# A quarter-row first load ahead of a streamed row sum

## Chip, cores and metric

One core of a Trainium2 chip. The metric is the device time of one execution in microseconds, the median of several runs of each kernel. The "span" of a profile (from the first to the last instruction of the program) is shorter than the time by about 1.4 us.

## The reference

```python
def reference(x):                       # x: 32 x 512 x 1024, float32
    relu_x = np.maximum(x, 0)
    return np.sum(relu_x, axis=-1)      # 32 x 512
```

64 MiB (67.11 MB) come in, 64 KB go out. There are 16,384 rows of 4 KB, 128 for each of the 128 SBUF partitions.

## The kernel before

Each partition owns 112 consecutive rows of a first region (pitch from partition to partition: 448 KB) and 16 rows of a second. The 112 rows arrive in seven chunks of 16 rows, 64 KB per partition, in three rotating buffers. All loads go through one queue, that of SyncE (SP). The first chunk is split into a one-row load and a fifteen-row load, and both are issued ahead of the barrier with which the program starts.

```python
CHUNKS = [[(0, 0, 1), (0, 1, 15)]] + [[(0, 16 * c, 16)] for c in range(1, 7)]
...
for c in range(NBIG + 1):
    if c >= NB:
        sp.wait_ge(s_dve, done[c - NB])       # buffer free again
    if c < NBIG:
        i = 0
        for g, j, n in CHUNKS[c]:
            sp.dma_start(
                out=buf[:, c % NB, i : i + n, :], in_=xv[g][:, j : j + n, :]
            ).then_inc(s_in[c], 16)
            i += n
            if c == 0:                        # moved ahead of the start barrier
                code.insert(arrival, code.pop())
                arrival += 1
... # tail loads of 8, 4, 2 rows and four pieces of the last two rows, then the first store
for c in range(NTWO):
    act.wait_ge(s_in[c], 16 * len(CHUNKS[c])) # for chunk 0: both loads
    ... # ScalarE applies ReLU in place, VectorE reduces along the row
```

## Time and profile before

| | before |
|---|---|
| median time, 6 runs | 161.05 us (160.93 to 161.22) |
| span of the profiled run | 159.5 us |
| load queue's share of 16 engines' span | 98.1% |
| VectorE / ScalarE busy | 76% / 64% |
| second load: landing after its issue | 21.3 us |

Two lines of the list of issues in the profile of the kernel before matter (columns: how many, KB, us from issue to landing):

```profile
buf<-in_x_dram SPq DMA_DIRECT2D x1, 7680.0 KB, 21.3
...
buf<-in_x_dram SPq DMA_DIRECT2D x1, 512.0 KB, 3.6
```

The first load is 128 packets of 4 KB, one per partition, eight for each of the 16 engines. The second is 128 packets of 60 KB, again eight per engine. These two lines are what the change resizes. The page, the chain and the windows follow in the prediction.

### The profile page before, as it was taken

To read this page: it belongs to the slowest core of one execution; us is meant where nothing else is said; L and a number is where in the kernel's file an instruction comes from. 1 tells how busy PE (TensorE), PEld (TensorE's weight loads), DVE (VectorE), ACT (ScalarE), POOL (GpSimd) and SP (SyncE) were. 2 spreads that over 40 slices of the span, in tenths; PEclk is the share of its full clock that TensorE was granted. 3 is DMA by queue.
4 is the path that set the end of the run, shared out by engine and by line. 5 is a ranking of instruction groups with operands and counts; after the bars stand their busy time and mean duration, and the time that the engine had idled before them with its cause. 6 is when DMAs were issued, how large, how long until landed. Compare 5 with 4: busy or idle time off the path is not lost.

```text
span 159.5 us, 149 instructions
## 1 busy us (share of the span) xinstructions
DVE 120.5 (76%) x59; ACT 101.5 (64%) x54; POOL 0.2 (0%) x4
## 2 busy tenths in 40 slices
DVE  0000000009999999999999999999999999898985
ACT  3000059990699808996099951999329980496975
POOL 0000000000000000000000000000000000000000
DMA  9969996996997998979969969969969979798994
GB/s 378 493 293 447 493 526 263 526 526 263 526 477 312 526 427 362 526 312 477 526 296 493 526 263 526 526 263 526 526 263 526 460 329 526 320 468 374 415 403 142
DMA packets 2449, 67.18 MB, mean 421 GB/s; under 512 B 528, under 2 KB 784, under 8 KB 1168
## 3 DMA queue, kind: packets, MB, share of 16 engines
q1 hardware_dynamic: 2448, 67.18, 98.1%
q14 instruction: 1, 0.01, 0.0%
HBM read 67.11 MB, written 0.07 MB: 421 GB/s over the span
## 4 chain that ended last, share of the span: by engine, by line
DVE 55%; DMA 34%; ACT 9%; SPq 2%; issue 0%
DVE res L156 54%; DMA buf<-in_x_dram 34%; ACT buf L141 9%; SPq L101 1%; SPq L112 1%; DVE buf L126 0%; DVE seam L126 0%; SPq L91 0%
## 5 line engine op out<-in xcount | busy, mean ns | idle before, releaser
L156 DVE TENSOR_REDUCE res<-buf 128x4 f32<-128x4096 f32 (+3 forms) x19 | 99.5, 5308 | 35.6 <-ACT buf L141 35.6
L141 ACT ACTIVATE buf<-buf 128x7168 f32<-128x7168 f32 (+5 forms) x13 | 80.4, 6233 | 46.2 <-DMA buf<-in_x_dram 46.2
L123 ACT ACTIVATE buf<-buf 128x1024 f32<-128x1024 f32 (+2 forms) x19 | 18.9, 998 | 8.9 <-DMA buf<-in_x_dram 8.9
L126 DVE TENSOR_SCALAR_CACHE_REDUCE buf<-buf 128x1024 f32<-128x1024 f32 (+2 forms) x19 | 20.7, 1142 | 1.9 <-DMA buf<-in_x_dram 1.9
L123 ACT ACTIVATION_READ_ACCUMULATOR buf<-buf 128x1 f32 x19 | 3.5, 187 | 0.0
L141 ACT ACT_TABLE_LOAD x1 | 1.3, 1283 | 1.3 <-PEq L216 1.3
L126 DVE DVE_READ_ACCUMULATOR buf<-buf 128x1 f32 x19 | 1.6, 82 | 0.0
L126 DVE TENSOR_SCALAR_CACHE_REDUCE seam<-seam 128x258 f32<-128x258 f32 x1 | 0.4, 423 | 0.0
L123 ACT ACTIVATE seam<-seam 128x130 f32<-128x130 f32 x1 | 0.3, 312 | 0.1
L123 ACT ACTIVATION_READ_ACCUMULATOR seam<-seam 128x1 f32 x1 | 0.2, 186 | 0.0
L216 POOL MEMSET const-bfloat16-1.0<- 128x1 bf16 x1 | 0.1, 101 | 0.0
L216 POOL MEMSET const-uint8-127<- 128x1 uint8 x1 | 0.1, 101 | 0.0
L216 POOL MEMSET const-float32-0.0<- 128x1 f32 x1 | 0.1, 98 | 0.2 <-issue 0.2
L216 POOL MEMSET const-float32-1.0<- 128x1 f32 x1 | 0.1, 98 | 0.0
L126 DVE DVE_READ_ACCUMULATOR seam<-seam 128x1 f32 x1 | 0.1, 83 | 0.0
## 6 DMA issues: line engine op xcount, KB each, us to landing
buf<-in_x_dram SPq DMA_DIRECT2D x1, 7680.0 KB, 21.3
buf<-in_x_dram SPq DMA_DIRECT2D x1, 4096.0 KB, 25.5
buf<-in_x_dram SPq DMA_DIRECT2D x1, 2048.0 KB, 30.0
buf<-in_x_dram SPq DMA_DIRECT2D x1, 1024.0 KB, 32.1
buf<-in_x_dram SPq DMA_DIRECT2D x1, 512.0 KB, 3.6
buf<-in_x_dram SPq DMA_DIRECT2D x1, 448.0 KB, 32.7
buf<-in_x_dram SPq DMA_DIRECT2D x1, 256.0 KB, 32.9
seam<-in_x_dram SPq DMA_DIRECT2D x1, 192.0 KB, 32.7
```

The source lines that it names most:

```text
L101: sp.dma_start(out=buf[:, tb, r : r + n, :], in_=xv[-1][:, r : r + n, :]).then_inc(s_in[NBIG + i], 16)
L112: sp.dma_start(out=flat[:, lo:hi], in_=rows[:, lo:hi]).then_inc(s_in[NBIG + len(TAIL) + k], 16)
L123: return act.activation(t, t, AF.Relu, accum_out=acc)
L126: return dve.tensor_scalar(out=t, in0=t, scalar1=0.0, scalar2=None, op0=ALU.max, op1=ALU.add, accum_out=acc)
L141: act.activation(t, t, AF.Relu).then_inc(s_act, 1)
L156: dve.tensor_reduce(out=res[:, c * BIG + r : c * BIG + r + n], in_=buf[:, c % NB, r : r + n, :], axis=X, op=ALU.add,).then_inc(s_dve, 1)
L216: nc = _bacc.Bacc("TRN2", target_bir_lowering=False, num_devices=1)
```

## The change

The intent is to let the bulk of the first chunk start sooner: the first load shrinks from a row (4 KB of each partition, 512 KB in all) to a quarter of a row (1 KB, 128 KB in all), and the second brings the other 63 KB as one run.

```diff
-CHUNKS = [[(0, 0, 1), (0, 1, 15)]] + [[(0, 16 * c, 16)] for c in range(1, 7)]
+CHUNKS = [[(0, 256), (256, BIG * D)]] + [[(16 * c * D, 16 * (c + 1) * D)] for c in range(1, 7)]
...
+    bulk = xv[0].rearrange("p j d -> p (j d)")
+    flat3 = buf[:, :, :, :].rearrange("p n j d -> p n (j d)")
...
-            i = 0
-            for g, j, n in CHUNKS[c]:
+            for lo, hi in CHUNKS[c]:
+                at = lo - BIG * D * c
                 sp.dma_start(
-                    out=buf[:, c % NB, i : i + n, :], in_=xv[g][:, j : j + n, :]
+                    out=flat3[:, c % NB, at : at + hi - lo], in_=bulk[:, lo:hi]
                 ).then_inc(s_in[c], 16)
-                i += n
```

## The prediction

> **What bounds the kernel now.** I read the page first, then the chain of waits in order of time, then the windows at the start, then the packet records behind them.
>
> ```profile
> span 159.5 us, 149 instructions
> ...
> DVE 120.5 (76%) x59; ACT 101.5 (64%) x54; POOL 0.2 (0%) x4
> ...
> DMA packets 2449, 67.18 MB, mean 421 GB/s; under 512 B 528, under 2 KB 784, under 8 KB 1168
> ...
> q1 hardware_dynamic: 2448, 67.18, 98.1%
> ```
>
> No compute engine comes near the span, but the one load queue keeps 16 engines busy for 98.1% of it. The chain in order of time seems to tell another story:
>
> ```profile
> 0.43 21.29 DMA buf<-in_x_dram
> ...
> 21.74 13.87 ACT buf L141
> ...
> 35.63 86.39 DVE res L156 x16
> ...
> 124.33 32.76 DMA buf<-in_x_dram
> ```
>
> VectorE owns over half of it, and that is a trap. The chain follows the semaphore that released each issue, not what kept the transfer waiting after the issue. The last loads are issued from 122.04, but the previous 8 MiB load lands near 137.8, so the queue has about 15 us of older work when they join it. The same holds earlier: the fourth 8 MiB load is issued at 52.99 and the third lands near 60.4. VectorE therefore has some 7 us of slack before the queue would run dry. The middle window confirms it:
>
> ```profile
> 1.30:2.00 0.70, 0.00 (x0) 0.70 (x1) 0.00 (x0) 1.00 0.66 140
> 2.00:2.70 0.70, 0.00 (x0) 0.54 (x1) 0.00 (x0) 1.00 0.94 380
> ...
> 20.80:136.90 116.10, 101.27 (x23) 82.46 (x17) 0.00 (x0) 1.00 1.00 434
> ```
>
> The columns are window, length, busy VectorE, ScalarE, GpSimd, the clock, the DMA share and GB/s. From 20.8 to 136.9 us the share is 1.00 at 434 GB/s: nothing can be gained there without fewer bytes. The input is 67.11 MB, which is 154.6 us at 434. The span is 159.5. So 4.9 us are outside full rate: about 1.0 before the first packet, about 2.0 after the last load lands (157.54 to 159.5, last sums and store), and the remaining 1.9 is a slow start, the small tail packets and the unevenness of the engines. Only the slow start is within reach of this change. The windows show it: 140 GB/s from 1.3 to 2.0, 380 from 2.0 to 2.7.
>
> **What the Trainium skill says.** "DMA: Bandwidth & Descriptors", section "Latency and other measured facts", puts the first byte of a hardware-generated DMA at about 600 ns and an HBM access at 0.2 us on average, up to 2 us at high load. The trace agrees in kind: the first packets start 1.0 us after the start of the first issue, 0.62 after its end, and take 0.16 to 0.87 us although 4 KB packets later take 0.159. The section "Rules for kernel authors" of that page asks for at least 1 MiB per DMA; the change goes from 512 KB to 128 KB in the first load, against that rule, but this load is followed without a wait by 7.9 MB, so I expect the rule's cost to stay hidden; the trace has such a case, the 128 KB load near the end, which runs back to back with its neighbours. "Perfetto Trace Analysis", section "Roofline", names about 435 GB/s as the ceiling of the 16 engines of one core; 434 measured says that the middle is at it.
>
> **The change part by part.**
> 1. The first load: 128 packets (8 per engine) shrink from 4,096 to 1,024 bytes. At the full rate the packet records give 155 ns from packet to packet at 4 KB. The 1 KB packets of the tail took 46 ns each in their records, and that load lands 0.35 us after the one before, 44 ns per packet. Removed per engine: 8 x 155 = 1.24 us; put in its place: 8 x 45 = 0.36 us. Net 0.88 us earlier.
> 2. The second load: the packets grow from 61,440 to 64,512 bytes. A 60 KB packet takes 2.267 us in its record, so 36.9 ns per KB; 3 KB x 8 packets add 8 x 0.111 = 0.89 us per engine. Net of 1 and 2: about zero. Bytes are the same, the number of DMAs and of packets is the same (one packet per partition and load already: 17 DMAs x (128 + 16) = 2448, as the page has it), and so is the number of issues.
> 3. Later loads: the same 64 KB runs under a flattened view. They are already one 64 KB packet per partition, 2.418 us each. I count 0.
> 4. The slow start. This is where sign and size come from. Per engine, the first load takes about 1.88 us on average (first packet near 1.11, first 60 KB packet near 2.99 in the packet records, range 2.73 to 3.25) where 1.24 would do, so 0.63 us are lost. All slow packets started before about 2.2 us, nearly all before 2.0; after that all take 0.159, and the 60 KB packets were never slow. If the loss belongs to the first two or three packets of an engine whatever their size, it stays, and the change is worth nothing. If it belongs to the time until 2.0 us, during which large packets would run well, a shorter first load lets the large ones in sooner and part of the 0.63 is saved. The second load is issued at 0.43 us; with the same 1.0 us lag its packets are possible from about 1.44. The first load then ends between 1.5 (no slow start) and 2.1 (all of the loss kept). Break-even is 2.99 - 0.89 = 2.10. So the gain lies between 0 and 0.6 us, and I take 0.15.
> Everything after the second load is a queue that never runs dry, so its gain reaches the end undiluted: 161.1 - 0.15 = 160.95 us.
>
> **The rivals.**
> - **Latency per packet.** Each small packet might pay the first packets' latency, about 0.48 us (in the window from 1.0 to 1.3 us a share of 1.61 x 0.3 us x 16 engines over 16 packets). Eight of them: 3.9 us, a loss of near 3 us, 164. Against it: in the kernel before, each engine's last five packets or so came every 155 ns, and small packets at both ends of the kernel run back to back. Unlikely, below 2%.
> - **A wait for descriptors of the second load.** If its packets were not ready when the first load ends, engines idle. For it: its issue starts only 0.43 us later, and today's long first load would hide a late arrival down to 2.7. Against it: the two result stores show all 128 packets started within 0.2 to 0.3 us, 0.84 us after the issue. If it comes, 0.2 to 0.5 us are lost: 161.4.
> - **The flattened view is cut into other packets.** Two 32 KB packets for one of 64 KB cost about 10 ns more each (9.72 us for eight 32 KB packets by their landings, against 19.35 for eight 64 KB): 48 per engine, 0.5 us. 4 KB packets would cost 16 x 155 - 2,418 = 62 ns each, 3 us in all. The kernel before has whole rows merged into one packet, so I see no reason for it: 3% for the first, less for the second.
> - **An earlier first step of compute.** None: ScalarE waits for both loads (21.74), and it has slack anyway.
>
> **Range and chances.** The three times of the kernel before span 160.94 to 161.22, so a median is good to 0.15 either way. Gain 0 to 0.6 with the lower half likelier, minus the descriptor rival: 160.4 to 161.4. Two per cent is 3.2 us, more than the whole loss at the start, so faster is nearly impossible; slower needs latency per packet or 4 KB packets.
>
> **What would show it.** Right: first load's landing falls from 3.6 us after issue to about 2.0 to 2.6; the second load lands at 21.3 to 21.7 (now 21.72); 2448 packets as before, share 1.00 and 434 GB/s in the middle; the end moves with the second load's landing. Step 4 is wrong if the GB/s between 1.3 and 2.0 stays near 140 with idle engines and large packets begin after 2.2. The whole is wrong if the middle rate changes, if the packet count grows, or if the second load lands later than 22.5 us.

## The result

| | before | changed |
|---|---|---|
| median time, 6 runs each | 161.05 us (160.93 to 161.22) | 161.32 us (161.17 to 161.57) |
| span of the profiled run | 159.5 us | 159.9 us |

The ratio is 1.0018 with a 95% interval of 1.0005 to 1.0031: the same within 2%, yet slower by an amount that stands clear of the noise.

The page of the changed kernel, the lines that answer to those shown of before:

```profile
span 159.9 us, 149 instructions
...
DVE 120.5 (75%) x59; ACT 101.5 (63%) x54; POOL 0.2 (0%) x4
...
DMA packets 2449, 67.18 MB, mean 420 GB/s; under 512 B 528, under 2 KB 912, under 8 KB 1168
...
q1 hardware_dynamic: 2448, 67.18, 97.9%
...
buf<-in_x_dram SPq DMA_DIRECT2D x1, 8064.0 KB, 21.7
...
buf<-in_x_dram SPq DMA_DIRECT2D x2, 128.0 KB, 17.4
```

Instructions, busy times and packet count are the same. Only the class of packets under 2 KB grew by 128, the first load. The last line is a trap of grouping: two loads of 128 KB, the first and one of the tail, stand in one row, and 17.4 us is the median of 2.1 and 32.8. The second load now lands 21.7 us after its issue instead of 21.3. The chain of waits in order of time says the same:

```profile
0.43 21.70 DMA buf<-in_x_dram
...
22.16 13.87 ACT buf L142
...
36.05 86.39 DVE res L157 x16
...
124.77 32.74 DMA buf<-in_x_dram
```

Every piece after the second load is as long as it was. The chain's last load ends at 157.51 against 157.09, so the 0.42 us that appear by 22.14 us (21.72 before) arrive at the end undiluted. All of the difference is in the first load pair. The windows of the changed kernel:

```profile
1.00:1.30 0.30, 0.00 (x0) 0.04 (x1) 0.00 (x0) 1.00 0.41 133
1.30:2.00 0.70, 0.00 (x0) 0.70 (x1) 0.00 (x0) 1.00 4.05 1328
2.00:2.70 0.70, 0.00 (x0) 0.54 (x1) 0.00 (x0) 1.00 0.69 276
20.80:136.90 116.10, 100.85 (x23) 82.46 (x17) 0.00 (x0) 1.00 1.00 434
```

The middle is untouched: share 1.00 and 434 GB/s. A share of 4.05 is no error: a packet is booked whole in the window in which it starts, so a window in which large packets start shows a share far above 1. That gives a way to read their length. Where a window holds the start of one large packet on each of the 16 engines and nothing else, share times window length is their mean time. The second round of large packets in the changed kernel is such a window:

```profile
4.60:5.20 0.60, 0.00 (x0) 0.00 (x0) 0.00 (x0) 1.00 3.98 1720
```

3.98 x 0.60 = 2.39 us for a 63 KB packet. The first round is mixed with small packets, so it has to be taken from the packet records of the trace:

```
us, means over the 16 engines      before   changed
first large packet starts           3.00      1.80
first large packet takes            2.27      3.05
later packets of that size take     2.27      2.38
third load (chunk 1) has landed    40.83     41.19
```

The large packets do start sooner, by 3.00 - 1.80 = 1.20 us. Eight packets of 63 KB instead of 60 KB cost 8 x (2.380 - 2.267) = 0.90 us more. That alone would be a gain of 0.30. But the first large packet of each engine takes 3.05 us instead of 2.38, a loss of 0.67. The sum is 0.37 us later; measured at the landing of chunk 1, 0.36.

### The profile page after: what moved, and what is told of

The parts are those of the page before. It is cut to its first block, busy times and chain, and to the rows that moved or that the text cites. A ratio compares the mean times of both kernels' runs of the same rounds, so it can differ in the third digit from the quotient of the medians.

```text
span 159.9 us, 149 instructions
## 1 busy us (share of the span) xinstructions
DVE 120.5 (75%) x59; ACT 101.5 (63%) x54; POOL 0.2 (0%) x4
## 4 chain that ended last, share of the span: by engine, by line
DVE 55%; DMA 34%; ACT 9%; SPq 2%; issue 0%
DVE res L157 54%; DMA buf<-in_x_dram 34%; ACT buf L142 9%; SPq L102 1%; SPq L113 1%; DVE buf L127 0%; DVE seam L127 0%; SPq L93 0%
## 6 DMA issues: line engine op xcount, KB each, us to landing
buf<-in_x_dram SPq DMA_DIRECT2D x1, 8064.0 KB, 21.7
buf<-in_x_dram SPq DMA_DIRECT2D x2, 128.0 KB, 17.4
```

## The experiments

Each ran beside the kernel before on the same chip. "Extra" is how much longer the first large packet of an engine took than later ones of its size, a mean of the 16 engines from the packet records (the records do not name the engine; the 16 that start earliest are taken as one for each). "Chunk 1" is the mean time over the engines at which the third issued load (64 KB per partition, the second in the runs without a small load) had landed. It can be compared between runs however the first 64 KB are cut.

```
run           first load   large start  extra  chunk 1   time (median)  ratio to before
(before)      4 KB            3.00      0.00    40.83    161.05
(changed)     1 KB            1.80      0.67    41.19    161.32         1.0018
row_flat      4 KB            3.03      0.01    40.87    160.99         1.0000
whole         none            1.22      0.65    40.89    161.01         0.9999
half_row      2 KB            2.12      0.27    40.80    160.89         0.9997
two_rows      8 KB            4.28      0.00    40.91    161.05         1.0002
late_second   1 KB            2.03      0.65    41.40    161.63         1.0042
late_others   1 KB            1.72      0.64    41.08    161.63         1.0044
early_others  1 KB            1.77      0.57    41.06    161.25         1.0015
pitch         1 KB            1.74      0.66    41.15    161.32         1.0019
reversed      1 KB, second    1.30      0.60    41.00    161.12         1.0004
eighth        512 B           1.75      0.64    41.26    161.34         1.0017
two_queues    1 KB, ScalarE   1.11      0.80    41.00    161.54         1.0021
after_first   1 KB, waited    3.26      0.79    42.76    163.00         1.0122
```

The start and chunk columns come from one profiled execution of each run, so small differences need a yardstick. Chunk 1 landed at 40.83 and 40.87 in the two runs with 4 KB first, and at 41.06 to 41.19 in the four runs whose 1 KB load and second load are issued as in the changed kernel (changed, `late_others`, `early_others`, `pitch`). A difference below some 0.1 us is therefore not a finding. Nor does chunk 1 decide the whole time: the traced execution of `half_row` was its slowest, 161.23 us, and had the earliest chunk 1, 40.80.

### The size of the first load

Two theories stood first. Theory A: something disturbs all transfers until about 2.2 us by the clock. Theory B: large packets that start cold are slow, and small packets ahead of them take the loss more cheaply. The diffs are against the changed kernel.

`row_flat`:

```diff
-CHUNKS = [[(0, 256), (256, BIG * D)]] + ...
+CHUNKS = [[(0, D), (D, BIG * D)]] + ...
```

> The changed kernel's flattened view with the old sizes (first load 4 KB of each partition, then 60 KB). If the size of the first load is the cause, this is the kernel before: 161.05 us within 0.15, the 60 KB packets 2.267 us each from the first on, second load landing at 21.7. If the flattened view is the cause, it is the changed kernel: 161.3 us.

160.99 us, ratio 1.0000 (0.9987 to 1.0012), and large packets at their steady length. The flattened view costs nothing; the size does.

`whole`:

```diff
+CHUNKS = [[(0, BIG * D)]] + ...
```

> One load of 64 KB of each partition, no small load ahead of it. Theory A, a disturbance by the clock (whatever moves before about 2.2 us is slow, by whatever size): the same bytes are lost as in the kernel before, so 161.0 to 161.1 us, or some less. Theory B, large packets that start cold and in step are slow and small ones ahead of them take the loss more cheaply: first 64 KB packets take 3 us or more against 2.42, and the time is at or above the changed kernel's, 161.3 to 161.7 us.

161.01 us, ratio 0.9999 (0.9986 to 1.0013). The first windows of this run hold the first and the second packet of every engine:

```profile
1.00:1.90 0.90, 0.00 (x0) 0.90 (x1) 0.00 (x0) 1.00 3.41 1165
3.90:4.65 0.75, 0.00 (x0) 0.00 (x0) 0.00 (x0) 1.00 3.22 1398
```

3.41 x 0.90 = 3.07 us for the first, 3.22 x 0.75 = 2.42 for the second. So large first packets pay 0.65 us as theory B says, but the time is that of the kernel before, as theory A says: all five executions (160.93 to 161.05) lie below all six of the changed kernel (161.17 to 161.57). Both expectations were half right, and theory B as I had it is refuted: the extra is the same as in the changed kernel, and still this kernel is not slower than before. A one-row first load is not shown to be worth anything against no first load at all, and a quarter row is worse than either.

`half_row` has `(0, 512), (512, BIG * D)`:

> First load 2 KB of each partition. Theory A: first large packets start near 2.2 us, little lost, 161.0 to 161.15 us. Theory B: between the two kernels, 161.1 to 161.3 us, with first large packets of 2.5 to 3 us against 2.34 at the steady rate.

160.89 us, ratio 0.9997 (0.9985 to 1.0010). Large packets start at 2.12 and the extra falls to 0.27; the small ones exceed their own median by 0.24 us per engine. The start-up loss is shared, not avoided: 0.27 + 0.24 = 0.51, against 0.56 in the 4 KB packets before. The time is the best median of all, but its five runs go from 160.80 to 161.23, so it is not shown to beat the kernel before.

`two_rows` has `(0, 2 * D), (2 * D, BIG * D)`:

> First load 8 KB of each partition, twice that of the kernel before. Both theories: large packets start after 3.5 us and run at 2.12 us each from the first on; 161.0 to 161.1 us. If longer small packets lose more in the start, up to 161.2; if less, 160.9.

161.05 us, ratio 1.0002 (0.9989 to 1.0014), as expected. From 4 KB up, the small packets take the loss and the large ones almost none (0.01 us at most).

### What the extra of the first large packets is not

`late_second` leaves the second load behind the start barrier:

```diff
-                if c == 0:
+                if c == 0 and lo == 0:
```

> The changed kernel with its 63 KB load issued after the start barrier, so about 0.85 us later; engines idle in between. Theory A (a disturbance until about 2.2 us by the clock): the first 63 KB packets start near 2.3 and take 2.38 us like the later ones, the second load lands near 22.0 and the time is 161.3 to 161.5 us. Theory B (large packets that start cold and in step): they still take 3 us or more on average, second load lands near 22.6, time 161.9 to 162.2 us.

The premise was off: the barrier let SP go at 0.78 us, so the issue moved by only 0.35 us and the large packets to 2.03. They still took 3.03 us, so theory A would need a disturbance that lasts longer than I had said. The time, 161.63 us, ratio 1.0042 (1.0028 to 1.0057), is later by about the delay.

`late_others` gives the first load its own semaphore and makes SP wait for it before the third load:

```diff
+        if c == 1:
+            sp.wait_ge(s_first, 16)
```

> The changed kernel with the third and fourth loads issued only when the first load has landed (its own semaphore), near 2.1 us instead of 1.27 and 1.64. If the issue of those loads (their descriptors) is what slows the first large packets, these shorten from a mean near 3.1 towards 2.4 to 2.7 us or the slow part moves, and the time falls to 160.7 to 161.1. If not, packets and time stay as in the changed kernel, 161.3.

The third and fourth issues moved from 1.27 and 1.64 us to 2.27 and 2.65; the extra stayed at 0.64. By itself this settles less than it was meant to: the moved issues still fall into the three microseconds that the first large packets take. The trace of the kernel before says more. Its later 8 MiB loads are issued at 52.99, 70.30, 87.55 and 104.79 us, in the midst of 64 KB packets, and no packet in flight in the 1.5 us from the start of such an issue took more than 2.44 us, against 2.42 for the rest. In the midst of a kernel, then, the issue of a load costs large packets nowhere near 0.64 us.

The time was 161.63 us with an interval of the ratio of 1.0020 to 1.0068, slower and with four runs scattered from 161.34 to 162.31. The record lists their spans: 160.0, 160.4, 160.3 and 160.2 us. So about 0.5 us of the slowest run lies outside the span (it is 1.9 us longer than its span, the others 1.3 to 1.4). The rest was not traced.

`early_others` issues all three chunks ahead of the barrier (`if c < NB:`):

> The reverse: third and fourth loads issued before the start barrier right behind the second, near 0.9 and 1.3 us. If their descriptors slow the first large packets, the time moves up to 161.5 or more or the slow part shifts earlier; if not, 161.3 as the changed kernel.

The issues came at 0.90 and 1.37 us; extra 0.57, 161.25 us, ratio 1.0015 (0.9998 to 1.0031). Not shown to differ from the changed kernel. This agrees with what was read off the later issues.

`pitch` reads the first chunk at 113 rows from partition to partition. Its output is wrong, which doesn't matter for the time.

```diff
+    other = xr[: 113 * P, :].rearrange("(p j) d -> p (j d)", p=P)
...
-in_=bulk[:, lo:hi]
+in_=(bulk if c else other)[:, lo:hi]
```

> The changed kernel with its first 64 KB of each partition read at a pitch of 113 rows (452 KB) instead of 112 (448 KB); wrong result on purpose. If the first large packets are slow because the partitions' runs, 448 KB apart, start in step on the same part of the memory, the packets shorten from near 3.1 to 2.4 to 2.8 us and the time falls to 160.7 to 161.1. If not, 161.3.

161.32 us, ratio 1.0019 (1.0004 to 1.0034), extra 0.66: no effect. This rules out only what a pitch of 452 KB instead of 448 KB would have cured.

`after_first` issues the 63 KB load when the 1 KB load has landed (own semaphore as in `late_others`, and the 63 KB load behind the start barrier):

```diff
+                if lo == 256:
+                    sp.wait_ge(s_first, 16)
```

> The changed kernel with the 63 KB load issued only when the 1 KB load has landed, near 2.1 us, so the large packets start near 3.2. If the 0.65 us that the first large packets lose belongs to a time of the kernel's start (now only possible if it lasts past 2.5 us), they run at 2.38 us each and the time is 162.0 to 162.2 us. If it belongs to large packets that start together on idle engines, they again take near 3.03 us and the time is 162.7 to 163.0 us.

163.00 us, ratio 1.0122 (1.0108 to 1.0135). In its windows, the first large packet of every engine starts in the first line and the second in the last:

```profile
3.05:3.70 0.65, 0.00 (x0) 0.44 (x1) 0.00 (x0) 1.00 4.88 1588
6.00:6.85 0.85, 0.00 (x0) 0.00 (x0) 0.00 (x0) 1.00 2.80 1214
```

4.88 x 0.65 = 3.17 us against 2.80 x 0.85 = 2.38. Packets that start at 3.1 to 3.6 us still pay, while the 60 KB packets of the kernel before, which start at 2.7 to 3.3 right behind 4 KB packets, do not. That ends theory A: the extra goes with large packets that begin without enough traffic ahead of them, not with a time. ScalarE's load of its function table is not the cause either: here it ran from 2.20 to 3.48, and the packet that started at 3.64 still took 2.95 us. In `late_second` it ran from 0.78 to 2.06, and the three packets that started at 2.06 to 2.14 took 3.03 to 3.11 us. The last issue of that stretch, too, had ended at 2.06.

The packet records show one thing more. An engine does not pay merely because the packet is its first. In `whole`, where nothing goes ahead of the large packets, the 13 that started by 1.27 us took 2.89 to 3.37 us, and the three at 1.53, 1.75 and 1.89 took 2.71, 2.88 and 2.42, the last no more than later packets. In `reversed` (below) the 11 that started by 1.23 us took 2.96 to 3.52, and the five at 1.64 to 1.96 only 2.39 to 2.81. This reads as a loss of what moves when the heavy traffic of all engines sets in, less for a packet that joins some 0.5 to 0.9 us later; no run was made to test it.

### Why 1 KB is worse than nothing

With the extra equal in `whole` and in the changed kernel, something else must cost the 0.3 us between them. The theory now, call it cover: the issue of the first load holds the second back by 0.43 us, and the 1 KB packets (8 KB per engine, 8 x 37.8 ns = 0.30 us of work at the steady rate) are too little to fill that. The terms from the packet records: against `whole` the large packets start 1.80 - 1.22 = 0.57 us later, are 1 KB shorter (8 x 0.038 = 0.30 saved), and the extra is 0.03 more. That makes 0.30 us; chunk 1 landed 0.30 later.

`reversed` issues the same two loads in the other order:

```diff
-CHUNKS = [[(0, 256), (256, BIG * D)]] + ...
+CHUNKS = [[(256, BIG * D), (0, 256)]] + ...
```

> The changed kernel with its two first loads in the other order: the 63 KB runs are issued at 0, the 1 KB ones behind them. Theory now (cover): the start-up loss of the first large packets, 0.65 us, is the same with and without a small load ahead, and the changed kernel loses because its 1 KB packets (8 KB per engine, 0.30 us of work) are used up before the second load, issued 0.43 us later, can deliver. Then the order alone repairs it: large packets start near 1.2 us on average, still 3.0 us long, and the time is 161.0 us, as with one load. Rival (the small packets themselves or the odd sizes cost it): 161.3 us as the changed kernel.

161.12 us against 161.09 for before in the same rounds, ratio 1.0004 (0.9992 to 1.0016). The windows of its first and second large packets:

```profile
1.00:2.00 1.00, 0.00 (x0) 0.75 (x1) 0.00 (x0) 1.00 2.98 1032
3.95:4.80 0.85, 0.00 (x0) 0.00 (x0) 0.00 (x0) 1.00 2.80 1214
```

2.98 us, then 2.38: the extra is still there, and still most of the loss is gone. The terms add up: large packets start 1.80 - 1.30 = 0.50 sooner, the 1 KB packets now come behind them (8 x 46 ns = 0.37), the extra is 0.07 less, in sum 0.20 sooner; chunk 1 landed 0.19 sooner. In time the interval leaves out the changed kernel's 1.0018 only just and overlaps that kernel's own interval, so it is the trace that carries this verdict. It carries it weakly: 41.00 is 0.06 below the earliest of the four 1 KB runs, and 0.11 above `whole`.

`eighth` halves the first load again, `(0, 128), (128, BIG * D)`:

> First load of 512 bytes of each partition, half of the changed kernel's. Cover: the second load still starts at about 1.65 to 1.8 us on average, and the first has moved 4 KB per engine less, 0.15 us of work: 161.4 to 161.5 us, worse than 1 KB although no small load at all gives 161.0. Rival (each small byte or packet costs, or the time goes smoothly to that of no small load): between 161.0 and 161.3 us.

161.34 us, ratio 1.0017 (1.0005 to 1.0030). Below the expected 161.4, and no different in time from 1 KB; chunk 1 lands at 41.26, 0.07 later than with 1 KB. Large packets start at 1.75, as early as with 1 KB though only half as much goes ahead of them: from a certain point the start is set by the second load's own issue, not by the first load's length. That fits cover. The rival, a smooth way from 1 KB down to none, would have put chunk 1 between 40.89 and 41.19; the 0.07 by which the run lies above is too little to exclude it alone.

`two_queues` has ScalarE issue the 1 KB load, so that SP can issue the 63 KB load at once (the rest of the edit, not shown, puts each issue ahead of its own engine's start barrier):

```diff
-                sp.dma_start(
+                (act if hi == 256 else sp).dma_start(
```

> The changed kernel with the 1 KB load issued by ScalarE's own queue, so that the issue of the 63 KB load on the SP queue is not held back by 0.43 us. Cover: large packets start near 1.2 to 1.4 us on average, the time is 160.9 to 161.1 us. Rival (the small load itself costs): 161.3 us. Were two queues slower to share the engines, also 161.3, but with large packets that start early.

Six runs fall into two groups, 161.05 and 161.07, and 161.50 to 161.74, with a ratio of 1.0021 (1.0007 to 1.0035). In time this misses the expected 160.9 to 161.1. But the spans of all six are 159.7 or 159.8 us, against 159.8 to 160.2 for the changed kernel and 159.5 to 159.9 for before in the same rounds: the slower group's 0.5 us lies outside the span, in what no profile shows.

The profile is of the 161.05 run: large packets start at 1.11 and chunk 1 lands at 41.00, as in `reversed`, which fits cover. It is not a test of a small load that goes ahead, though. By the packet records the 1 KB packets, issued at 0.12 us, started only at 4.16, behind the first large packets, and then 16 at a time, once between every two rounds of large packets, up to 21.4 us. The run repeats `reversed` by other means.

## Why the prediction was right or wrong

The time, 161.32 us, lies in the range of 160.4 to 161.4, and "within 2%" was right. The sign of the small difference was not: 0.15 us of gain were expected, 0.27 of loss came. That the range held is partly luck: its lower part rested on large packets that run well at the start, and they did not; its upper end had been set for a late second load, which is only a part of what came (below).

- **The bound** was read rightly: the middle stayed at 434 GB/s, VectorE's long chain did not matter, and a shift at the second load's landing arrived at the end in full (0.42 us at both places of the profiled runs).
- **Parts 1 to 3** hold. The 1 KB packets took 46 ns in the median, the 63 KB packets 2.38 us, and `row_flat` shows the view to be free. One unit slipped: 36.9 ns is for 1,000 bytes, and the added 3 KB are 3,072, so the 0.89 us should read 0.91; measured 0.90.
- **Part 4** failed, and with it the sign. The step that failed is the one that kept the large packets out of the slow start. From "the 60 KB packets were never slow" it took that the loss of 0.63 us belongs either to an engine's first few packets or to the time until 2.0 us, "during which large packets would run well", and the gain of 0 to 0.6 us rested on the second case. The large packets did begin before its break-even of 2.10, at 1.80. But they did not run well: 0.67 us were lost in the first packet of each engine, on average. The loss went over from the small packets to the large ones. In the 4 KB packets of before it was 0.56 us (1.83 of which 1.27 are steady work); in the changed kernel it was 0.01 in the 1 KB packets and 0.67 behind them. So the case "it stays, and the change is worth nothing" came nearest; another 0.12 us of loss, and some 0.2 us for which the engines stood idle between the two loads, turned nothing into a loss.
- **The signs** were not sharp enough. "Right" was also to be shown by the second load landing at 21.3 to 21.7; it landed at 22.14, inside the 22.5 that would have overturned the whole. The sign set for part 4 (a rate that stays near 140 GB/s, large packets after 2.2 us) did not show, at 1328 GB/s and 1.80 us, and yet part 4 was wrong: it asked when large packets start and not how long they take.
- **The rival of a wait for the second load** was there, though small: the earliest large packets came 1.13 us after the start of their issue, against 1.02 for the first load, and the engines were done with the first load at about 1.6 us (an estimate: its mean landing at 1.95, less the 0.37 us by which chunk 1's landings follow the ends of its packets), while the large packets began at 1.80. Together with the 0.43 us of the issue this is, by the account of cover, what makes 1 KB worse than no first load.
- **Latency per packet**, 164 us, did not come: eight 1 KB packets took 0.38 us of an engine's time.

What the extra of the first large packets is remains open. It is not the clock time, the issue of the later loads, ScalarE's table load or a pitch of exactly 448 KB. It is absent behind eight 4 KB packets per engine and 0.27 us behind eight of 2 KB, and it is smaller for packets that start after the others. Whether it arises where the data are read or where they are written was not tested. No run is shown to beat the kernel before.

## What to carry to other kernels

When one load clears the way for a larger one, compare its transfer time with the issue time of the next: here 0.30 us of work could not cover 0.43 us of issue. Leaving the small load out was better by 0.3 us; issuing it second was better by 0.2 in the trace, and in time not clearly. A loss seen on small packets at the start of a kernel need not be theirs; take the small ones away once and see whether the loss goes or moves to the packets behind them. If a change touches only the ramp, size the ramp first: here it was 0.6 us of 161, so no cut of it could pass 2%.

## What the Trainium skill lacked or had wrong

- "DMA: Bandwidth & Descriptors" has no slow start of large packets. Here the first packets of 63 to 64 KB took, in the mean of 16 engines, 0.57 to 0.80 us more than the 2.38 to 2.42 of later ones whenever nothing larger than 1 KB packets went ahead, and at most 0.01 us more behind eight 4 KB packets per engine.
- The same page, section "Latency and other measured facts", gives about 600 ns to the first byte without saying from where. Counted from the end of the issue, 0.62 us agrees; counted from its start it was 1.01 us, and 1.13 us for the second load of the changed kernel.
- The same page, section "Issuing engines are not separate DMA queues", calls the time to initiate a DMA "usually small relative to the DMA itself". An issue on the SP queue took 0.33 to 0.45 us in most cases here, more than the 0.30 us of work in the 128 KB load. By the account above, which is in part argued, that is why this load is worse than none.
